# An encoder trunk in fp32: 16 of 22 feed-forward pairs by seven products, and the residual kept in DRAM meanwhile

## The chip, the cores and the metric

The kernel runs on one core of a Trainium2 chip. The metric is the time of one execution on the device in microseconds. The core's engines work side by side, each from its own queue of instructions: TensorE (PE) multiplies matrices, VectorE (DVE) and ScalarE (ACT) do elementwise work, GpSimd (POOL) a little of that, and SyncE (SP) issues most of the transfers from DRAM. The four compute engines see the on-chip memory SBUF; matmuls write to PSUM banks of 128 x 512 fp32.

## The reference: what is computed

A bidirectional encoder of two layers, 512 positions, width 1024. Each layer has two feed-forward half-steps, so there are four of them in the run, and they are what the change touches:

```python
def rmsnorm(x, g):
    xf = x.astype(jnp.float32)
    y = xf * lax.rsqrt(jnp.mean(xf * xf, axis=-1, keepdims=True) + RMS_EPS)
    return (y * g.astype(jnp.float32)).astype(x.dtype)

def swiglu(x, w_gate, w_up, w_down):
    return (jax.nn.silu(x @ w_gate) * (x @ w_up)) @ w_down

    for i in range(DEPTH):
        h = h + 0.5 * swiglu(rmsnorm(h, norm_ffn1[i]), ffn1_w_gate[i], ffn1_w_up[i], ffn1_w_down[i])
        # a mixer: windowed and dilated attention (layer 0), 2-D neighbourhood attention (layer 1)
        h = h + 0.5 * swiglu(rmsnorm(h, norm_ffn2[i]), ffn2_w_gate[i], ffn2_w_up[i], ffn2_w_down[i])
        gate = jax.nn.sigmoid(rmsnorm(h, norm_ple[i]) @ w_ple_gate[i])
        h = h + gate * (p[i] @ w_ple_proj[i])
    return rmsnorm(h, norm_final)
```

The hidden width of the feed-forward is 2816 = 22 x 128.

## The kernel before

Everything lies feature-major: a chunk is 128 features by 512 positions, and the residual h is eight chunks. Precision comes from splitting: every operand is a high part, rounded by ACT (`split`, L123), and a low part, the difference, formed by DVE (L124). A product is three matmuls: high by high, high by low, low by high (`mm3`, L144 to L146).

A feed-forward stage (`ffn`) first goes through 22 pairs. Pair m is 128 columns of the gate and the same 128 of the up matrix: two weight units of 128 x 1024, 512 KB each, which SP loads into a pool of four raw slots (`wr`) and ACT and DVE split into `wh` and `wl`. There are three kinds of pair.

- `pair_front` (m = 0, 1, 2) multiplies the chunks of h times the norm's gain, before the row scale R is known, and multiplies the result by R afterwards (L236, L238). R comes out of squares (L177), a sum over chunks (L182, on POOL), a column sum on PE, a power on POOL and a spread through PE (L208) to ACT (L216).
- `pair` (m = 3, 4 and 15 to 21) multiplies the normalised chunks y: 48 matmuls of 512 columns.
- `pair_fast` (m = 5 to 14) uses the Strassen-Winograd scheme: the 2 x 2 block product (gate and up, by the two halves of the features, by the two halves of the positions) by seven half-size products in place of eight, 84 matmuls of 256 columns. Its weights come as `rs` (one load, and a second one from POOL's queue that adds onto it), `ra` and `rb`; sums of them are formed on DVE (L310, L311) and split. On the other side it needs eight sums of halves of y, `t`, made by `sums` (L276 to L287). Products 1 and 2 go to the two halves of one bank, whose sum is formed by a copy on ACT (L330) and an add on DVE (L331) under high priority; product 5 then accumulates onto the first of them, so it must come after L331. Product 6 uses the split of rb.

The normalised y is formed chunk by chunk by `normal` (L265) after pairs 0 and 1, four chunks each; `sums` forms the same x again from h, gain and R (L276), two of four after pair 2 and two after pair 3. Each result of a pair is split into two slots of the pool `act`. After the pairs the down projection takes three weight units per output chunk, eight outputs, each added to h with a factor 0.5 (L381); the next stage's norm is begun for each chunk as it comes.

Pools set what may be under way at once: 9 slots of residual, 57 of act, 8 of tmp, 4 each of raw, high and low weights. A scheduler orders the instructions of each engine when the program is built, mainly by the program's order and by when slots come free, with some instructions raised by a priority; within an engine the order is then fixed. So the order on DVE, where nearly every split and sum queues, is a product of the pools' sizes as well.

## Time and profile before

| | |
|---|---|
| median of 3 runs | 2135.37 us (2133.22 to 2135.96) |
| the profiled execution | 2134.86 us, span 2133.1 us |
| matmuls on PE | 11390 |
| busy: PE, DVE, ACT, POOL | 97%, 60%, 43%, 14% of the span |
| read from DRAM, written | 223.42 MB, 2.59 MB |

A row of a timeline has the start in us, the duration in us, the engine, the line, the operation, the tiles written and read, and in brackets how long the engine had been idle before it and which instruction ended that. A duration reaches from issue to the end, so those of matmuls overlap; their pace is the distance of two starts. A row of the view by windows has the window, its length, then busy time and count for PE, the weight loads (PEld), DVE, ACT and POOL, the granted PE clock, the share of the DMA engines' time and GB/s. A row of the view of waits has who waited for whom, the total in us, the number of times, the longest.

### The profile page before, as it was taken

The numbers are of one execution on the slowest core, as the hardware profiler recorded it, in microseconds if no ns is written. First come the engines' busy times: TensorE is split into PE (matmuls) and PEld (weight loads), VectorE is DVE, ScalarE is ACT, GpSimd is POOL, SyncE is SP. The second block draws the span as 40 slices with busy tenths as digits, with TensorE's granted clock in tenths as the row PEclk, the third lists the DMA queues.
The fourth block names the chain that finished last, engine by engine and source line by source line (L and its number), as shares of the span: only waits on it lengthen the run. The fifth ranks groups of instructions, "written<-read, shape, count | busy, mean of one in ns | idle before, by whom it ended". The sixth has DMA issues, their size and how long they took to land.

```text
span 2133.1 us, 29295 instructions
## 1 busy us (share of the span) xinstructions
PE 2064.9 (97%) x11390; PEld 1781.0 (83%) x11390; DVE 1289.2 (60%) x2269; ACT 916.2 (43%) x1519; POOL 291.6 (14%) x212
## 2 busy tenths in 40 slices
PE   8999999999999999999999999999999999999998
PEld 6898888777787799888887998888888879988886
DVE  8875332699786887333359873333778777743334
ACT  5454222465534455322344552223656545532232
POOL 3000001233212100001111000013222210000111
PEclk9999999999999999999999999999999999999999
DMA  6574333221222366333333753334333236633331
GB/s 186 133 175 131 91 93 102 85 75 55 65 69 90 88 166 165 109 94 94 106 99 96 181 159 97 92 99 124 103 105 103 81 85 167 164 109 90 101 106 49
DMA packets 86922, 233.71 MB, mean 110 GB/s; under 512 B 18176, under 2 KB 25856, under 8 KB 86784
## 3 DMA queue, kind: packets, MB, share of 16 engines
q1 hardware_dynamic: 80736, 210.78, 32.9%
q0 software_dynamic: 5760, 20.97, 6.0%
q8 instruction: 89, 1.46, 0.3%
q14 instruction: 49, 0.40, 0.1%
q10 hardware_dynamic: 288, 0.10, 0.0%
HBM read 223.42 MB, written 2.59 MB: 106 GB/s over the span
## 4 chain that ended last, share of the span: by engine, by line
PE 76%; DVE 12%; ACT 3%; DMA 3%; issue 2%; POOL 2%; SPq 0%; POOLq 0%; DVEq 0%; ACTq 0%
PE mm L145 10%; PE mm L146 10%; PE mm L144 10%; PE sc L146 7%; PE sc L144 7%; PE sc L145 7%; PE mm L321 3%; PE mm L323 3%; PE mm L322 3%; DVE wl L124 3%; DVE act L124 2%; PE sc L321 1%; PE sc L322 1%; PE sc L323 1%; DMA wr<-in_gu_dram 1%
## 5 line engine op out<-in xcount | busy, mean ns | idle before, releaser
L123 ACT ACTIVATE wh<-wr 128x1024 fp32r<-128x1024 f32 (+1 forms) x400 | 415.0, 1041 | 784.8 <-PE mm L145 286.3
L124 DVE TENSOR_TENSOR wl<-wr,wh 128x1024 fp32r<-128x1024 f32 (+1 forms) x383 | 468.7, 1224 | 385.6 <-ACT wh L123 382.6
L145 PE MATMUL mm<-act,wh 128*128 128x512 f32 x1240 | 485.0, 391 | 2.6 <-DVE act L171 1.6
L144 PE MATMUL mm<-act,wh 128*128 128x512 f32 x1240 | 484.7, 391 | 1.1 <-ACT wh L123 0.8
L146 PE MATMUL mm<-act,wl 128*128 128x512 f32 x1240 | 483.8, 390 | 0.5 <-DVE wl L124 0.5
L146 PE MATMUL sc<-act,wl 128*128 128x512 f32 x818 | 320.3, 392 | 12.4 <-DVE wl L124 12.4
L144 PE MATMUL sc<-act,wh 128*128 128x512 f32 x818 | 320.5, 392 | 0.0
L145 PE MATMUL sc<-act,wh 128*128 128x512 f32 x818 | 320.1, 391 | 0.0
L145 PEld LDWEIGHTS mm<-act,wh 128*128 128x128 f32 x1240 | 233.1, 188 | 51.8 <-DVE act L171 5.1
L144 PEld LDWEIGHTS mm<-act,wh 128*128 128x128 f32 x1240 | 233.1, 188 | 47.7 <-ACT wh L123 1.6
L146 PEld LDWEIGHTS mm<-act,wl 128*128 128x128 f32 x1240 | 233.1, 188 | 46.0 <-DVE wl L124 1.0
L182 POOL TENSOR_TENSOR ssq<-ssq,tmp 128x512 f32<-128x512 f32 x55 | 90.6, 1646 | 977.4 <-ACT tmp L177 950.5
L321 PE MATMUL mm<-act,wh 128*128 128x256 f32 x640 | 183.7, 287 | 15.6 <-DVE tmp L331 15.6
L146 PEld LDWEIGHTS sc<-act,wl 128*128 128x128 f32 x818 | 154.8, 189 | 45.7 <-DVE wl L124 13.6
L145 PEld LDWEIGHTS sc<-act,wh 128*128 128x128 f32 x818 | 154.7, 189 | 32.2
L323 PE MATMUL mm<-act,wl 128*128 128x256 f32 x640 | 181.1, 283 | 0.0
L144 PEld LDWEIGHTS sc<-act,wh 128*128 128x128 f32 x818 | 154.8, 189 | 31.5
L322 PE MATMUL mm<-act,wh 128*128 128x256 f32 x640 | 181.0, 283 | 0.0
L321 PEld LDWEIGHTS mm<-act,wh 128*128 128x128 f32 x640 | 122.6, 192 | 20.3 <-DVE tmp L331 19.6
L123 ACT ACTIVATE act<-tmp 128x512 fp32r<-128x512 f32 x156 | 95.4, 625 | 75.3 <-POOL tmp L239 38.8
L322 PEld LDWEIGHTS mm<-act,wh 128*128 128x128 f32 x640 | 122.7, 192 | 0.2
L323 PEld LDWEIGHTS mm<-act,wl 128*128 128x128 f32 x640 | 122.7, 192 | 0.2
(183 smaller groups left out, 3008.4 us busy)
## 6 DMA issues: line engine op xcount, KB each, us to landing
wr<-in_gu_dram SPq DMA_DIRECT2D x176, 512.0 KB, 3.7
wr<-in_dn_dram SPq DMA_DIRECT2D x64, 512.0 KB, 3.5
wr<-in_gu_dram POOLq DMA_DIRECT2D x40, 512.0 KB, 6.6
wr<-in_dn_dram SPq DMA_DIRECT2D x32, 384.0 KB, 3.1
tmp<-in_gu_dram SPq DMA_DIRECT2D x40, 256.0 KB, 4.3
wr<-in_qk_ab_dram SPq DMA_DIRECT2D x20, 512.0 KB, 3.5
wr<-in_plg_dram SPq DMA_DIRECT2D x16, 512.0 KB, 3.5
wr<-in_qk_c_dram SPq DMA_DIRECT2D x16, 512.0 KB, 3.8
```

The lines of the kernel that those rows point to most:

```text
L123: self.nc.scalar.activation(hi, src, AF.Copy)
L124: (lo_eng or self.nc.vector).tensor_tensor(lo, src, hi.bitcast(F32), op=ALU.subtract)
L144: mm(out, stat[0], mov[0], start=start, stop=False)
L145: mm(out, stat[0], mov[1], start=False, stop=False)
L146: mm(out, stat[1], mov[0], start=False, stop=stop)
L182: eng.tensor_tensor(self.acc, self.acc, sq, op=ALU.add)
L321: mm(out, w[0][:, c], xs[k][0][:, x], start=start and k == 0, stop=False, skip_group_check=True)
L322: mm(out, w[0][:, c], xs[k][1][:, x], start=False, stop=False, skip_group_check=True)
L323: mm(out, w[1][:, c], xs[k][0][:, x], start=False, stop=stop and k == half - 1, skip_group_check=True)
```

## The change

In a feed-forward stage pairs 0 to 3 are now front pairs, 4 and 5 plain, and 6 to 21 go by seven products, 16 in place of 10. `halves(c)` takes the place of `normal` and `sums`: it forms x for chunks c and c + 4 once and makes y[c], y[c + 4] and t[c] from it; it is called after each of the pairs 0 to 3. The raw weight pool has a fifth slot. The residual moves into the act pool, 64 slots; at the start of a stage it is written to DRAM (`kept`; in the first stage the input is there already), and each chunk is loaded again in the down projection. In a front pair the product of gate and up goes from POOL to DVE. In a pair by seven products rb's load is first in the code; the results of products 4 and 6 share a bank, so that two adds of 256 columns (L340, L341) become one of 512 (L353). At the start of the program the first weight unit is loaded in two pieces, the identity matrix later and without its bf16 copy, all eight splits of the input stand ahead of the squares, and the squares are summed on DVE. The mixers' code stays, apart from one tile that moves to the act pool.

```diff
@@ constants and pools
-FRONT = 3
-FAST = 5, 15
+FRONT = 4
+FAST = range(6, 22)
+SUMS = 0, 1, 2, 3
+FIRST = 2
+ACTS = 64
+WR = 5
...
-        self.hp = pool("hres", 9)
-        self.ap_ = pool("act", 57)
+        self.ap_ = pool("act", ACTS)
         self.tp = pool("tmp", 8)
-        self.wr = pool("wraw", 4)
+        self.wr = pool("wraw", WR)
@@ setup
         self.ident = self.cp.tile([P, P], F32, name="ident")
-        nc.scalar.dma_start(self.ident, io["ident"])
-        self.identb = self.cp.tile([P, P], BF16, name="identb")
-        nc.vector.tensor_copy(self.identb, self.ident)
...
-        idle = self.cp.tile([P, T], BF16, name="idle")
+        idle = self.small("R", [P, T], BF16, bufs=1)
...
-        self.h = [None] * KC
+        self.h = []
+        w = io["gu1"][0, 0]
+        units = [(w[:, (1 - j) * UNIT:(2 - j) * UNIT], self.unit_tiles()) for j in range(2)]
+        pieces = {0: (0, 0, UNIT // 4), 1: (0, UNIT // 4, UNIT), 2: (1, 0, UNIT)}
         self.begin_norm(0)
-        for c in range(KC):
-            self.h[c] = self.hp.tile([P, T], F32, tag="h", name=self.nm("h"))
-            nc.sync.dma_start(self.h[c], io["xT"][:, c, :])
-            self.norm_split(c)
-            if c in (0, 2):
-                self.ahead.append(self.unit(io["gu1"][0, 0, :, (1 - c // 2) * UNIT:(2 - c // 2) * UNIT]))
+        for n in range(KC + FIRST):
+            if n < KC:
+                self.h.append(self.act())
+                nc.sync.dma_start(self.h[n], io["xT"][:, n, :])
+                if n in pieces:
+                    j, a, b = pieces[n]
+                    nc.sync.dma_start(units[j][1][0][:, a:b], units[j][0][:, a:b])
+            c = n - FIRST
+            if c >= 0:
+                self.norm_split(c)
+                if c in pieces:
+                    j, a, b = pieces[c]
+                    self.split(*(x[:, a:b] for x in units[j][1]))
+        self.ahead = [u[1:] for _, u in units]
+        nc.sync.dma_start(self.ident, io["ident"])
@@ norm_square
-        nc.scalar.activation(sq, self.h[c], AF.Square)
+        ins = nc.scalar.activation(sq, self.h[c], AF.Square)
+        if self.k == 0:
+            self.tc.keep_in_program_order(ins)
...
-            eng = nc.vector if c == KC - 1 and self.k else nc.gpsimd
+            eng = nc.vector if c == KC - 1 or self.k == 0 else nc.gpsimd
@@ pair_front
-        nc.gpsimd.tensor_tensor(t2, t1, t2, op=ALU.mult)
+        nc.vector.tensor_tensor(t2, t1, t2, op=ALU.mult)
@@ normal and sums become halves
-    def sums(self, y, c):
+    def halves(self, c):
         nc, H = self.nc, T // 2
-        v = []
+        v, out = [], []
         for k in (c, c + KC // 2):
             x = self.tmp()
             nc.vector.scalar_tensor_tensor(x, self.h[k], self.gain[:, self.k, k:k + 1], self.R, op0=ALU.mult, op1=ALU.mult)
+            out.append(self.split_chunk(x, nc.vector))
             v += [x[:, :H], x[:, H:]]
...
-        return [self.split_chunk(x, nc.vector) for x in (s, r)]
+        return (*out, [self.split_chunk(x, nc.vector) for x in (s, r)])
@@ pair_fast
+        dma(rb, w[:, :M])
         dma(rs, w[:, M:M + UNIT])
         nc.gpsimd.dma_start(rs, w[:, :UNIT], accum_op=ALU.add)
         dma(ra, w[:, UNIT:])
-        dma(rb, w[:, :M])
...
-        ab, cd, eb = self.bank(), self.sbank(), self.obank()
-        pa, pb, pc, pd, pe = ab[:, l], ab[:, r], cd[:, l], cd[:, r], eb[:, l]
+        ab, ed, cb = self.bank(), self.sbank(), self.obank()
+        pa, pb, pc, pe, pd = ab[:, l], ab[:, r], cb[:, l], ed[:, l], ed[:, r]
...
-        tt(up[:, l], pe, xy[:, r], op=ALU.add)
-        tt(up[:, r], pd, xy[:, r], op=ALU.add)
+        two = lambda x: x.rearrange("p (a x) -> p a x", a=2)
+        tt(two(up), two(ed), xy[:, r].unsqueeze(1).broadcast_to([P, 2, H]), op=ALU.add)
@@ ffn
+        if first:
+            kept = io["xT"].rearrange("p c t -> c p t")
+        else:
+            kept = self.dp.tile([KC, P, T], F32, name=f"kept_{i}_{which}")
+            for c in range(KC):
+                nc.sync.dma_start(kept[c], self.h[c])
...
-            elif FAST[0] <= m < FAST[1]:
+            elif m in FAST:
...
-            if m < FRONT - 1:
-                n = KC // (FRONT - 1)
-                for c in range(m * n, m * n + n):
-                    y[c] = self.normal(c)
-            elif FRONT - 1 <= m < FAST[0] - 1:
-                n = KC // 2 // (FAST[0] - FRONT)
-                for c in range((m - FRONT + 1) * n, (m - FRONT + 2) * n):
-                    t[c] = self.sums(y, c)
+            for c, after in enumerate(SUMS):
+                if m == after:
+                    y[c], y[c + KC // 2], t[c] = self.halves(c)
         self.begin_norm(k_next)
         for m in range(KC):
+            for c in range(m + 1 if m else 0, min(m + 2, KC)):
+                self.h[c] = self.act()
+                nc.sync.dma_start(self.h[c], kept[c])
```

The lines of the two versions answer to each other so: splits L123, L124 become L136, L137; `mm3` L144 to L146 becomes L160 to L162; L170, L171 become L186, L187; L177, L182 become L193, L200; L216 becomes L234; the front pair's L236, L238, L239 become L254, L256, L257; L276 becomes L287; loads L297 to L300 become L309 to L312; the matmuls of the seven products L321 to L323 become L333 to L335; L330, L331 become L342, L343; L345 becomes L357; L381 becomes L398.

On DVE, within the pairs by seven products of the first stage, the order before reads as follows. L345 ends a pair, `wl<-tmp` is the low part of rb, `wl<-wr` that of a unit of a later product or pair, `act` that of the pair's result:

```order
L124 TENSOR_TENSOR wl_238_1215<-wr_230_1197,wh_237_1214 128x1024
L343 TENSOR_TENSOR tmp_225_1096<-sc_223_1094,tmp_225_1096 128x256
L345 SCALAR_TENSOR_TENSOR tmp_225_1096<-tmp_226_1097,tmp_225_1096 128x512
L124 TENSOR_TENSOR wl_240_1219<-tmp_232_1199,wh_239_1218 128x512
L124 TENSOR_TENSOR wl_253_1334<-wr_249_1326,wh_252_1333 128x1024
L331 TENSOR_TENSOR tmp_244_1225<-mm_241_1222,tmp_244_1225 128x256
L124 TENSOR_TENSOR act_229_1194<-tmp_225_1096,act_228_1193 128x512
L310 TENSOR_TENSOR wr_249_1326<-wr_249_1326,wr_250_1327 128x512
L311 TENSOR_TENSOR wr_249_1326<-wr_249_1326 128x512
```

In this pair two splits stand between L345 and L331; in the next one it is one:

```order
L124 TENSOR_TENSOR wl_257_1344<-wr_249_1326,wh_256_1343 128x1024
L343 TENSOR_TENSOR tmp_244_1225<-sc_242_1223,tmp_244_1225 128x256
L345 SCALAR_TENSOR_TENSOR tmp_244_1225<-tmp_245_1226,tmp_244_1225 128x512
L124 TENSOR_TENSOR wl_259_1348<-tmp_251_1328,wh_258_1347 128x512
L331 TENSOR_TENSOR tmp_263_1354<-mm_260_1351,tmp_263_1354 128x256
L124 TENSOR_TENSOR act_248_1323<-tmp_244_1225,act_247_1322 128x512
```

The wide split `wl_272` stands behind L331 there. The same place after the change, two pairs that follow each other:

```order
L357 SCALAR_TENSOR_TENSOR tmp_268_1403<-tmp_269_1404,tmp_268_1403 128x512
L137 TENSOR_TENSOR act_272_1500<-tmp_268_1403,act_271_1499 128x512
L343 TENSOR_TENSOR tmp_287_1531<-mm_284_1528,tmp_287_1531 128x256
L137 TENSOR_TENSOR wl_283_1525<-tmp_275_1505,wh_282_1524 128x512
L137 TENSOR_TENSOR wl_296_1639<-wr_292_1631,wh_295_1638 128x1024
L322 TENSOR_TENSOR wr_292_1631<-wr_292_1631,wr_293_1632 128x512
L137 TENSOR_TENSOR wl_298_1643<-wr_293_1632,wh_297_1642 128x1024
L351 TENSOR_TENSOR tmp_289_1533<-ob_286_1530,tmp_289_1533 128x256
L323 TENSOR_TENSOR wr_292_1631<-wr_292_1631 128x512
L353 TENSOR_TENSOR tmp_288_1532<-sc_285_1529,tmp_289_1533 128x512
L137 TENSOR_TENSOR wl_300_1649<-wr_292_1631,wh_299_1648 128x1024
L355 TENSOR_TENSOR tmp_287_1531<-sc_285_1529,tmp_287_1531 128x256
```

In the first pair only the result's split is ahead of L343, and rb's has moved behind it. The second pair has rb's and a wide one ahead again:

```order
L357 SCALAR_TENSOR_TENSOR tmp_287_1531<-tmp_288_1532,tmp_287_1531 128x512
L137 TENSOR_TENSOR wl_302_1653<-tmp_294_1633,wh_301_1652 128x512
L137 TENSOR_TENSOR wl_315_1767<-wr_311_1759,wh_314_1766 128x1024
L343 TENSOR_TENSOR tmp_306_1659<-mm_303_1656,tmp_306_1659 128x256
L137 TENSOR_TENSOR act_291_1628<-tmp_287_1531,act_290_1627 128x512
L322 TENSOR_TENSOR wr_311_1759<-wr_311_1759,wr_312_1760 128x512
```

This is the order of seven of the sixteen pairs (11, 13, 15 and 17 to 20); in the others no wide split is ahead of L343, and the order is the same in all four stages.

Also on DVE, the end of the work on the normalised halves in the first stage, ahead of the pairs by seven products. Before, `wl_149` is the second unit of pair 4, behind both of the last sums:

```order
L276 SCALAR_TENSOR_TENSOR tmp_136_596<-h_30_174,gain_93,R_43_253 128x512
L124 TENSOR_TENSOR act_134_591<-tmp_130_581,act_133_590 128x512
L283 TENSOR_TENSOR tmp_137_598<-tmp_135_594 128x256
L285 TENSOR_TENSOR tmp_138_599<-tmp_136_596,tmp_135_594 128x256
L284 SCALAR_TENSOR_TENSOR tmp_137_598<-tmp_137_598,tmp_136_596 128x256
L124 TENSOR_TENSOR wl_149_645<-wr_147_643,wh_148_644 128x1024
L286 SCALAR_TENSOR_TENSOR tmp_138_599<-tmp_137_598,tmp_136_596 128x256
L124 TENSOR_TENSOR act_140_605<-tmp_137_598,act_139_604 128x512
L124 TENSOR_TENSOR wl_158_689<-wr_154_681,wh_157_688 128x1024
```

After, the split in that place is that of the second unit of pair 3, a front pair, with two of the last four splits of halves behind it:

```order
L296 SCALAR_TENSOR_TENSOR tmp_107_485<-tmp_107_485,tmp_104_479 128x256
L137 TENSOR_TENSOR act_103_476<-tmp_101_473,act_102_475 128x512
L297 TENSOR_TENSOR tmp_108_486<-tmp_104_479,tmp_101_473 128x256
L137 TENSOR_TENSOR act_106_482<-tmp_104_479,act_105_481 128x512
L298 SCALAR_TENSOR_TENSOR tmp_108_486<-tmp_107_485,tmp_104_479 128x256
L137 TENSOR_TENSOR wl_119_532<-wr_117_530,wh_118_531 128x1024
L137 TENSOR_TENSOR act_110_492<-tmp_107_485,act_109_491 128x512
L254 TENSOR_TENSOR tmp_121_561<-mm_116_505,R_44_251 128x512
L137 TENSOR_TENSOR act_112_496<-tmp_108_486,act_111_495 128x512
```

From R's first use (L236, L254) there are 59 rows to the first of these splits (`wl_149`) and 40 to the second (`wl_119`).

On SP, the loads for the pairs by seven products, before (L297 rs, L299 ra, L300 rb; their tiles are numbered upwards from pair to pair):

```order
L299 DMA wr_192_939<-in_gu1_dram 128x1024
L297 DMA wr_212_1069<-in_gu1_dram 128x1024
L300 DMA tmp_175_812<-in_gu1_dram 128x512
L299 DMA wr_211_1068<-in_gu1_dram 128x1024
L297 DMA wr_231_1198<-in_gu1_dram 128x1024
L300 DMA tmp_194_941<-in_gu1_dram 128x512
L299 DMA wr_230_1197<-in_gu1_dram 128x1024
```

After (L310 rs, L312 ra, L309 rb):

```order
L312 DMA wr_178_863<-in_gu1_dram 128x1024
L310 DMA wr_198_992<-in_gu1_dram 128x1024
L312 DMA wr_197_991<-in_gu1_dram 128x1024
L309 DMA tmp_161_737<-in_gu1_dram 128x512
L310 DMA wr_217_1120<-in_gu1_dram 128x1024
L312 DMA wr_216_1119<-in_gu1_dram 128x1024
L309 DMA tmp_180_865<-in_gu1_dram 128x512
L310 DMA wr_236_1248<-in_gu1_dram 128x1024
```

A pair's rb stood between rs and ra of two pairs later; it now stands behind both of them.

21 lines of the change are left out of this document (9 added, 12 removed).

## The prediction

> **What bounds the kernel now.** I read the busy shares first, then the chain that ended last, then TensorE's (PE's) waits over the whole run.
>
> ```profile
> PE 2064.9 (97%) x11390; PEld 1781.0 (83%) x11390; DVE 1289.2 (60%) x2269; ACT 916.2 (43%) x1519; POOL 291.6 (14%) x212
> PE 76%; DVE 12%; ACT 3%; DMA 3%; issue 2%; POOL 2%; SPq 0%; POOLq 0%; DVEq 0%; ACTq 0%
> ...
> PE mm L321 <- DVE tmp L331: 15.6, 17, 1.4
> PE sc L146 <- DVE wl L124: 12.4, 4, 3.7
> ...
> PE mm L145 <- DVE act L171: 1.6, 4, 0.7
> ```
>
> PE is busy 97% of the span and holds 76% of the chain, so time goes down in two ways only: fewer or shorter matmuls, or less of PE waiting. The two largest waits both end on VectorE (DVE) inside the feed-forward stages, and both stand at places that the change rewrites: the copy-and-add L331 in the pairs by seven products, and the low part of a weight unit (L124) just ahead of them.
>
> The pace of the matmuls comes from the timeline of PE, from the first and the last row of an unbroken run of each kind.
>
> ```profile
> 32.21 0.39 PE L145 MATMUL mm<-act,wh 128*128 128x512 f32 x1
> ...
> 41.95 0.39 PE L146 MATMUL mm<-act,wl 128*128 128x512 f32 x1
> ...
> 81.03 0.28 PE L321 MATMUL ob<-act,wh 128*128 128x256 f32 x1
> ...
> 88.35 0.28 PE L322 MATMUL sc<-act,wh 128*128 128x256 f32 x1
> ```
>
> The first two are 43 matmuls apart: 9.74 / 43 = 0.2265 us each. The others are 61 apart: 7.32 / 61 = 0.120 us. A plain pair has 48 of the wide ones, 10.87 us; a pair by seven products has 84 of the narrow ones, 10.08 us. Each pair that changes kind saves 0.80 us of PE, if nothing new waits.
>
> **The pairs by seven products, as they run now.** They do not run at 10.08. The first row below is one of the matmuls that waited, the second the next such, two pairs later; the third is that stretch by engine.
>
> ```profile
> 122.26 0.39 PE L321 MATMUL mm<-act,wh 128*128 128x256 f32 x1 [1.20 <-DVE tmp L331]
> ...
> 143.79 0.39 PE L321 MATMUL mm<-act,wh 128*128 128x256 f32 x1 [1.11 <-DVE tmp L331]
> ...
> 122.00:143.70 21.70, 20.42 (x168) 20.21 (x168) 17.33 (x28) 11.73 (x19) 1.71 (x2) 1.00 0.70 171
> ```
>
> Two pairs take 143.79 - 122.26 = 21.53 us against 20.16: 1.37 lost, of which 1.1 shows as a wait and the rest is a slow restart. With 15.6 us in the view of waits, that scales to 15.6 x 1.37 / 1.11 = 19; by the sum of all start-to-start gaps above 0.120 it is 21 us over 40 pairs, 0.53 a pair, the figure I use. It is not throughput: in the same stretch DVE works 17.33 of 21.70. It is order. Product 5 may not start before L331 has read its bank, 4 x 12 x 0.120 = 5.76 us after the pair's start. The timeline of DVE shows a pair that kept this date and the next, that missed it:
>
> ```profile
> 107.87 0.69 DVE L345 SCALAR_TENSOR_TENSOR tmp<-tmp,tmp 128x512 f32<-128x512 f32 x1 [0.70 <-ACT tmp L344]
> 109.42 0.69 DVE L124 TENSOR_TENSOR wl<-tmp,wh 128x512 fp32r<-128x512 f32 x1 [0.85 <-ACT wh L123]
> 110.03 0.42 DVE L331 TENSOR_TENSOR tmp<-mm,tmp 128x256 f32<-128x256 f32 x1
> ...
> 118.64 0.69 DVE L345 SCALAR_TENSOR_TENSOR tmp<-tmp,tmp 128x512 f32<-128x512 f32 x1 [0.70 <-ACT tmp L344]
> 119.70 0.69 DVE L124 TENSOR_TENSOR wl<-tmp,wh 128x512 fp32r<-128x512 f32 x1 [0.36 <-ACT wh L123]
> 120.64 1.23 DVE L124 TENSOR_TENSOR wl<-wr,wh 128x1024 fp32r<-128x1024 f32 x1 [0.26 <-ACT wh L123]
> 121.79 0.42 DVE L331 TENSOR_TENSOR tmp<-mm,tmp 128x256 f32<-128x256 f32 x1
> ```
>
> The second has a 1.23 us split of the next unit ahead of L331. Ahead of that stands the split of rb, which waits for its hi part on ScalarE (ACT), and that for a load:
>
> ```profile
> 114.65 1.07 SPq L300 DMA_DIRECT2D tmp<-in_gu_dram  x1
> ...
> 119.03 0.63 ACT L123 ACTIVATE wh<-tmp 128x512 fp32r<-128x512 f32 x1 [0.42 <-DMA tmp<-in_gu_dram]
> ```
>
> Issued at 114.65, used at 119.03: 4.4 us. So the chain is rb's load, ACT, two splits, L331.
>
> **The change, part by part.** (a) *Start.* Now the first pair waits for the low parts of x (L171, the 1.6 us above and the slow run of DVE behind it).
>
> ```profile
> 0.00:24.50 24.50, 20.09 (x60) 10.76 (x61) 17.62 (x17) 15.73 (x23) 11.80 (x11) 0.93 0.64 223
> ...
> 7.39 0.50 PE L144 MATMUL mm<-act,wh 128*128 128x512 f32 x1 [0.79 <-ACT wh L123]
> ...
> 24.35 0.40 PE L146 MATMUL sc<-act,wl 128*128 128x512 f32 x1
> 24.58 0.61 PE L189 MATMUL tr<-ones,ssq 128*128 128x1 f32 x5
> ...
> 6.61 0.74 DVE L171 SCALAR_TENSOR_TENSOR act<-h,gain,act 128x512 fp32r<-128x512 f32 x1
> ...
> 13.10 8.57 DVE L171 SCALAR_TENSOR_TENSOR act<-h,gain,act 128x512 fp32r<-128x512 f32 x5
> ...
> 12.24 8.87 POOL L182 TENSOR_TENSOR ssq<-ssq,tmp 128x512 f32<-128x512 f32 x5 [0.15 <-ACT tmp L177]
> ...
> 29.13 0.69 DVE L236 TENSOR_TENSOR tmp<-mm,R 128x512 f32<-128x512 f32 x1 [2.26 <-ACT R L216]
> ...
> 14.28 0.61 ACT L177 ACTIVATE tmp<-h 128x512 f32<-128x512 f32 x1
> ...
> 15.93 0.71 ACT L170 ACTIVATE act<-h,gain 128x512 fp32r<-128x512 f32 x1
> ...
> L123 ACT ACTIVATE wh<-wr 128x1024 fp32r<-128x1024 f32 (+1 forms) x400 | 415.0, 1041 | 784.8 <-PE mm L145 286.3
> ```
>
> One L171 alone takes 0.74; five beside GpSimd's (POOL's) L182 take 8.57, 1.71 each, while ACT had its last part ready at 16.64. The change takes L182 off POOL and puts the squares behind the splits. The five then cost 5 x 0.74 = 3.7, 4.9 less, and the squares' 0.61 us each leave ACT's way. Without waits, 48 matmuls from 7.39 end at 18.3; the pair now ends at 24.35 + 0.23 = 24.6. I take -6; if x's arrival decides (the share of DMA is 0.64 here) -2; at best -7.5, with an earlier start from the first weights' smaller piece. The identity matrix, now loaded behind part of x, is wanted only for spreading R, after 25; the cast that is dropped stood beside other work.
> The Trainium skill, "SBUF — State Buffer", section "Who interferes with whom", says that a VectorE instruction with two SBUF inputs contends with a GpSimd instruction that reads SBUF. L171 and L182 are such a pair, and 0.74 against 1.71 agrees; by that rule the seven adds on DVE give the 4.9 back in full, the upper part of my term.
>
> (b) *Entry.* Four times the pairs by seven products begin late, behind DVE's queue after the scale R is known:
>
> ```profile
> 68.31 0.50 PE L146 MATMUL sc<-act,wl 128*128 128x512 f32 x1 [1.93 <-DVE wl L124]
> ...
> 698.31 0.60 ACT L216 ACTIVATE R<-tr 128x512 f32<-128x512 f32 x1
> ...
> 740.00 0.58 PE L146 MATMUL sc<-act,wl 128*128 128x512 f32 x1 [3.16 <-DVE wl L124]
> 740.37 0.63 PE L144 MATMUL sc<-act,wh 128*128 128x512 f32 x1
> ...
> 699.00:740.00 41.00, 37.84 (x170) 31.21 (x168) 37.02 (x62) 20.92 (x31) 6.32 (x5) 1.00 0.34 84
> 740.00:744.00 4.00, 4.00 (x11) 3.14 (x12) 4.00 (x6) 0.63 (x1) 0.00 (x0) 0.57 0.45 131
> ```
>
> From R to the end of that window DVE has 62 instructions, 37.02 us, 0.60 each; PE's 170 matmuls last 38.5. The wait is followed by 4.00 us at a granted clock of 0.57 with 11 starts in them, ten intervals in place of 17.6: 7.6 x 0.2265 = 1.7 us more. 12.4 + 3 x 1.7 = 17.5; by start-to-start gaps 2.2, 5.3, 5.1 and 5.5, together 18. After the change each x is formed once and split once, and the queue from R to the low part of the second unit of pair 3, the split that now stands behind this work, is 40 instructions: 40 x 0.60 = 24, with one wide split and more 0.69s 26 us. PE has 128 matmuls in that time, 29 us. Stages 2 to 4 lose 0.4 each, for the last y. In the first stage R comes late: 8 splits, 8 squares and 3 weight parts on ACT (8 x 0.71 + 8 x 0.61 + 3 x 1.04 = 13.7, from about 7) end near 20.7; the last add, 0.7, and the 29.13 - 24.58 = 4.55 that the steps from the sum to R take now put it near 26, 3 us sooner, while the first pair ends 6 sooner. Of PE's 29 us of cover 8 are then gone, 21 against 26, less the 2 us or so that PE loses by itself while it waits for R: 3.5 us of wait are left there. 18 - 4.7 = 13.3 gained; ends 0 (DVE is no sooner) and 17. The product of gate and up, moved from POOL to DVE, adds 0.69 a pair, counted in the 26; uncovered it would be 4 x 4 x 0.69 = 11.
>
> (c) *Kind of pair.* 6 more in each of 4 stages, 24 x 0.80 = -19.2.
> By the Trainium skill, "TensorE: Matmul & The Clock Gate", section "Back-to-back issue gap", the isolated gap is N/2.4 + 2.5 ns, 215.8 and 109.2 ns for these widths: an estimate of 24 x 1.19 = -28.5 in place of -19.2, and a time near 2081. No chance is given to it, since both intervals stand measured above at a granted clock of 1.00.
>
> (d) *Waits in these pairs.* 40 x 0.53 = 21 become 64 x s. The new order has the wide split ahead of the copy-and-add (now L343) in pairs 11, 13, 15 and 17 to 20: seven in sixteen, against four in ten. But the fifth raw slot lets the big loads go about 8 us sooner, so those splits no longer wait for their data; rb is issued behind the ra of two pairs on. With the durations above I replayed DVE's queue in its new order: in a row of pairs with the wide split ahead, the copy-and-add ends 4.2 to 4.6 us after the pair's start, within 5.76; where such a pair follows one without it, 0 to 0.5 late. One add of 512 columns for two of 256 saves 2 x 0.42 - 0.69 = 0.15 a pair. POOL issues its accumulating load for 24 more pairs; it is busy 1.71 of 21.70 and has lost its adds, so nothing is queued ahead of them. My replay leaves out jitter of the loads, so I take s = 0.2, 12.8 us: -8. Ends: s = 0.05, -18; s = 0.53 as now, +13.
>
> (e) *The residual in DRAM.* Three times eight 256 KB writes at a stage's start and four times eight reads in the down projection, two outputs ahead at the start and one later. A down stage has room:
>
> ```profile
> 255.00:355.00 100.00, 100.00 (x443) 82.79 (x442) 32.32 (x34) 27.28 (x33) 9.05 (x5) 1.00 0.32 96
> ```
>
> A load of that size, rb's, took 4.4 us; an output's 66 matmuls are 15 us. If one came late, it would first delay L398 on DVE, then the norm's chunks queued behind it. A write waits for its own chunk; SP's loads behind it are for pairs two later. I count nothing; uncovered, 4.4 us for each stage's first read, at most 18. For the passage from pair 21, whose delayed splits now stand together, I add 1.5 (0 to 6).
>
> Sum: -6 - 13.3 - 19.2 - 8 + 1.5 = -45.0. The profiled execution took 2134.9 (span 2133.1), the median is 2135.4: **2090**. Own range, 2078 to 2100.
>
> **The rivals.** *B: the waits stay.* Order alone decides, and s is 0.53: 64 x 0.53 - 12.8 = 21 more, **2111**. For it: more wide splits stand ahead of the copy-and-add. Against: what the rows show waiting there is the data of rb and the wide unit, and both loads move. *C: the waits go* (s = 0.05, 9.6 less; the entries at their best, 3.7 less): **2077**. *D: slower.* The tmp slots run out. The results of pairs 16 to 20 stay in tmp until the act slots are free, so eight of eight are taken when rb of pair 21 is wanted; if rb's load is issued only when its product is due, each such pair waits 4.4 + 0.63 + 0.69 = 5.7 us. From 45 / 5.7 = 8 pairs in all on nothing is gained; with 16 (pairs 18 to 21 of each stage) +91, **2181**. Against: by count they fit. *E: the entries stay as they are*, since the halves' instructions run slower in one row than the mean 0.60: 13.3 back, **2103**.
>
> **How the numbers follow.** Forecast 0.54, B 0.19, C 0.12, D 0.08, E 0.07. B, C and E all lie on the faster side; of D a quarter ends near no change. A measurement of this kernel tells about 0.2% (4 us) from no change: faster 0.92, same 0.02, slower 0.06. The range of 8 in 10 takes in E, B and most of C: 2073 to 2113.
>
> **What would show it.** In the changed profile: the first pair ends near 18 and L186's mean is near 0.74; the wait of PE for a weight's low part falls from 12.4 to under 5; the wait for L343 is 5 to 15 us over 64 pairs, with two pairs 20.2 to 20.8 us apart; PE's matmuls rise by 24 x 36 = 864; no wait on L391. The forecast is wrong if two pairs still take 21.5, or if waits on rb's split appear at pairs 18 to 21.

## The result, and the profile after

The changed kernel takes 2110.6 us (median of 4 runs, 2109.96 to 2113.26) against 2134.3 for the one before on the same chip: ratio 0.9891, 95% interval 0.9874 to 0.9908. It is 23.7 us faster. The forecast was 45 us, 2090. The sign held, and the time lies inside the range of 8 in 10 (2073 to 2113) but outside the forecast's own (2078 to 2100); the gain is about half of the one forecast.

Of the page and the view of TensorE's waits, the rows that answer to those shown before:

```profile
PE 2043.4 (97%) x12254; PEld 1807.9 (86%) x12254; DVE 1382.1 (66%) x2416; ACT 983.8 (47%) x1640; POOL 282.7 (13%) x217
PE 84%; DVE 8%; issue 4%; ACT 3%; POOL 1%; DMA 1%; SPq 0%; DVEq 0%; ACTq 0%; POOLq 0%
...
PE mm L333 <- DVE tmp L343: 25.1, 19, 2.6
...
PE mm L160 <- ACT act L186: 2.5, 1, 2.5
...
PE sc L162 <- DVE wl L137: 0.7, 1, 0.7
```

The matmuls rose by 864, as the change says. The wait at the entry of the pairs by seven products fell from 12.4 us to 0.7. The wait for the copy-and-add, now L343, did not fall: 25.1 us in 19 waits, where it was 15.6 in 17. Summed over the gaps between starts above 0.120 us, the 64 pairs lose 9.5, 8.2, 5.7 and 10.6 us in the four stages, 34.0 together or 0.53 a pair, the rate before the change. Two pairs that still take 21.5 us were named as a sign that the forecast is wrong: two take 21.4, 21.3, 20.9 and 21.6 us in the mean of the four stages, and 22.9 in the stretch below.

One of the longest of these waits, in pair 11 of the first stage, which starts at 132.0, by the timelines of SP, POOL, ACT, DVE and PE:

```profile
131.05 0.33 SPq L312 DMA_DIRECT2D wr<-in_gu_dram  x1
131.43 0.50 SPq L309 DMA_DIRECT2D tmp<-in_gu_dram  x1
...
129.06 0.86 POOL L311 DMA_DIRECT2D wr<-in_gu_dram  x1 [10.99 <-DMA wr<-in_gu_dram]
...
137.20 0.63 ACT L136 ACTIVATE wh<-tmp 128x512 fp32r<-128x512 f32 x1 [1.81 <-DMA tmp<-in_gu_dram]
...
135.42 0.69 DVE L357 SCALAR_TENSOR_TENSOR tmp<-tmp,tmp 128x512 f32<-128x512 f32 x1 [0.70 <-ACT tmp L356]
137.87 0.69 DVE L137 TENSOR_TENSOR wl<-tmp,wh 128x512 fp32r<-128x512 f32 x1 [1.75 <-PE sc L334]
138.81 1.22 DVE L137 TENSOR_TENSOR wl<-wr,wh 128x1024 fp32r<-128x1024 f32 x1 [0.25 <-ACT wh L136]
139.95 0.42 DVE L343 TENSOR_TENSOR tmp<-mm,tmp 128x256 f32<-128x256 f32 x1
...
140.43 0.38 PE L333 MATMUL mm<-act,wh 128*128 128x256 f32 x1 [2.46 <-DVE tmp L343]
...
132.00:154.90 22.90, 20.44 (x170) 20.24 (x170) 17.57 (x25) 12.31 (x19) 1.73 (x2) 1.00 0.65 170
```

rb's load goes out 0.38 us behind ra, 0.6 ahead of the pair's start, and ACT has it at 137.20, 5.8 us later; in the pair shown before the change it was 4.4 us. DVE has nothing to do from 136.1 to 137.9, since its next instruction is the split of rb, and the wide split and L343 stand behind it. The bracket at 137.87 names a matmul, but ACT's high part of rb ended at 137.83; in all the pairs where this split waits, it starts 0.03 us after ACT's end. L343 ends 8.4 us after the pair's start, and its date is 5.76. The window by engines shows that DVE had time enough: 17.57 of 22.90.

This pair is one of the worst. In the traces as a whole, rb's split and a wide one stand ahead of L343 in the 28 pairs 11, 13, 15 and 17 to 20 of the four stages, and these lose 29 of the 34 us, 1.0 each. In them rb lands 3.5 us after the pair's start in the mean (2.0 to 5.3), and where L343 is late it ends 3.2 us after the landing. Before the change 16 pairs had that order; rb landed 3.5 us after the start there too, and they lost 15 us, 0.95 each. So such a pair is no worse than before, and there are more of them. Pairs 7 to 9 and 21 have rb's split alone ahead of L343 and lose next to nothing. Pair 6 has both splits ahead, which the section on the change leaves out, but its rb lands 0.8 to 2.5 us before the pair's start, and L343 is in time in all four stages. In the first, where pair 6 starts at 81.41:

```profile
85.50 1.22 DVE L137 TENSOR_TENSOR wl<-wr,wh 128x1024 fp32r<-128x1024 f32 x1 [1.74 <-ACT wh L136]
86.64 0.42 DVE L343 TENSOR_TENSOR tmp<-mm,tmp 128x256 f32<-128x256 f32 x1
```

The start, by the timelines of PE, DVE and ACT, and the entry of the first stage:

```profile
9.62 0.79 PE L160 MATMUL mm<-act,wh 128*128 128x512 f32 x1 [2.46 <-ACT act L186]
...
15.52 0.63 PE L161 MATMUL mm<-act,wh 128*128 128x512 f32 x1
15.94 0.60 PE L162 MATMUL mm<-act,wl 128*128 128x512 f32 x1
...
12.34 2.07 DVE L187 SCALAR_TENSOR_TENSOR act<-act,gain,act 128x512 fp32r<-128x512 f32 x3
...
22.92 0.68 DVE L200 TENSOR_TENSOR ssq<-ssq,tmp 128x512 f32<-128x512 f32 x1
...
27.31 0.95 PE L207 MATMUL tr<-ones,ssq 128*128 128x1 f32 x8
...
31.22 0.60 ACT L234 ACTIVATE R<-tr 128x512 f32<-128x512 f32 x1 [0.37 <-PE tr L226]
...
55.71 0.50 PE L162 MATMUL sc<-act,wl 128*128 128x512 f32 x1 [0.68 <-DVE wl L137]
```

PE starts early, runs out of data, waits 2.46 us, and then has its matmuls 0.43 apart until 16, at a granted clock of 0.50. The 48th wide matmul of the program starts at 23.2 (24.3 before), the 96th at 36.5 (37.9 before): 1.1 to 1.4 us gained. In the profiles of six of the kernels below, which have the same start, the 96th comes at 35.0 to 36.8, so this place scatters by nearly 2 us. R is ready at 31.8, later than the 29.1 before: the last square is added at 23.6, but the matmuls that sum it over the partitions (L207) stand in PE's queue behind the first seventeen of pair 1 and run at 27.31.

The residual's way through DRAM shows in no wait. The down stage runs as it did, PE busy without a gap:

```profile
255.00:355.00 100.00, 100.00 (x443) 82.83 (x442) 32.14 (x34) 27.74 (x34) 9.05 (x5) 1.00 0.39 122
```

### The profile page after: what moved, and what is told of

Same layout as the page of the kernel before. It is cut to its first block, busy times and chain, and to the rows that moved or that the text cites. A ratio compares the mean times of both kernels' runs of the same rounds, so it can differ in the third digit from the quotient of the medians.

```text
span 2108.2 us, 31604 instructions
## 1 busy us (share of the span) xinstructions
PE 2043.4 (97%) x12254; PEld 1807.9 (86%) x12254; DVE 1382.1 (66%) x2416; ACT 983.8 (47%) x1640; POOL 282.7 (13%) x217
## 4 chain that ended last, share of the span: by engine, by line
PE 84%; DVE 8%; issue 4%; ACT 3%; POOL 1%; DMA 1%; SPq 0%; DVEq 0%; ACTq 0%; POOLq 0%
PE mm L161 9%; PE mm L162 9%; PE mm L160 9%; PE sc L160 6%; PE sc L162 6%; PE sc L161 6%; PE mm L333 6%; PE mm L335 6%; PE mm L334 6%; PE sc L333 3%; PE sc L334 3%; PE sc L335 3%; PE ob L333 1%; PE ob L334 1%; PE ob L335 1%
## 5 line engine op out<-in xcount | busy, mean ns | idle before, releaser
L136 ACT ACTIVATE wh<-wr 128x1024 fp32r<-128x1024 f32 (+2 forms) x425 | 441.5, 1040 | 659.9 <-PE mm L161 210.0
L137 DVE TENSOR_TENSOR wl<-wr,wh 128x1024 fp32r<-128x1024 f32 (+2 forms) x408 | 496.5, 1219 | 339.5 <-ACT wh L136 333.9
L160 PE MATMUL mm<-act,wh 128*128 128x512 f32 (+1 forms) x1048 | 410.9, 393 | 2.8 <-ACT act L186 2.5
L161 PE MATMUL mm<-act,wh 128*128 128x512 f32 (+1 forms) x1048 | 411.2, 392 | 1.1 <-POOL act L137 0.6
L162 PE MATMUL mm<-act,wl 128*128 128x512 f32 (+1 forms) x1048 | 410.0, 391 | 0.0
L333 PE MATMUL mm<-act,wh 128*128 128x256 f32 x1024 | 293.6, 287 | 25.4 <-DVE tmp L343 25.1
L335 PE MATMUL mm<-act,wl 128*128 128x256 f32 x1024 | 290.0, 283 | 0.0
L334 PE MATMUL mm<-act,wh 128*128 128x256 f32 x1024 | 289.9, 283 | 0.0
L162 PE MATMUL sc<-act,wl 128*128 128x512 f32 x626 | 243.7, 389 | 0.7 <-DVE wl L137 0.7
L160 PE MATMUL sc<-act,wh 128*128 128x512 f32 x626 | 244.3, 390 | 0.0
L161 PE MATMUL sc<-act,wh 128*128 128x512 f32 x626 | 243.9, 390 | 0.0
L160 PEld LDWEIGHTS mm<-act,wh 128*128 128x128 f32 x1048 | 197.8, 189 | 41.8 <-ACT act L186 2.9
L161 PEld LDWEIGHTS mm<-act,wh 128*128 128x128 f32 x1048 | 197.9, 189 | 41.4 <-DVE act L137 1.8
L162 PEld LDWEIGHTS mm<-act,wl 128*128 128x128 f32 x1048 | 197.7, 189 | 37.8
L333 PEld LDWEIGHTS mm<-act,wh 128*128 128x128 f32 x1024 | 196.4, 192 | 30.7 <-DVE tmp L343 30.3
L334 PEld LDWEIGHTS mm<-act,wh 128*128 128x128 f32 x1024 | 196.7, 192 | 0.2
L335 PEld LDWEIGHTS mm<-act,wl 128*128 128x128 f32 x1024 | 196.6, 192 | 0.0
L200 POOL TENSOR_TENSOR ssq<-ssq,tmp 128x512 f32<-128x512 f32 x48 | 79.2, 1649 | 696.8 <-ACT tmp L193 670.2
L334 PE MATMUL sc<-act,wh 128*128 128x256 f32 x512 | 145.5, 284 | 0.0
L333 PE MATMUL sc<-act,wh 128*128 128x256 f32 x512 | 145.5, 284 | 0.0
L335 PE MATMUL sc<-act,wl 128*128 128x256 f32 x512 | 145.4, 284 | 0.0
```

The lines of the kernel that those rows point to most:

```text
L136: self.nc.scalar.activation(hi, src, AF.Copy)
L137: (lo_eng or self.nc.vector).tensor_tensor(lo, src, hi.bitcast(F32), op=ALU.subtract)
L160: mm(out, stat[0], mov[0], start=start, stop=False)
L161: mm(out, stat[0], mov[1], start=False, stop=False)
L162: mm(out, stat[1], mov[0], start=False, stop=stop)
L200: eng.tensor_tensor(self.acc, self.acc, sq, op=ALU.add)
```

## The experiments

**Where the 34 us come from.** Theory 1: rb lands late, its split stands ahead of the copy-and-add in DVE's queue. Theory 2: the wide split, or the amount of work on DVE. The first edit takes rb out of the tmp pool:

```diff
+        self.wb = pool("wrb", 2)
...
-        rb = self.tmp()
+        rb = self.wb.tile([P, T], F32, tag="rb", name=self.nm("rb"))
```

> The changed kernel with one edit: rb gets a pool of two slots of its own, so that its load no longer waits for a tmp slot, and SP issues it a pair earlier; rb's split is then done before the end of the pair ahead, and only the wide split of the next unit stands ahead of L344 (the copy-and-add, L343 in the change). Theory 1 (the waits come from rb's late landing, its split standing ahead of the copy-and-add): the 25.1 us of waits fall under 5, the 34 us lost in the pairs by seven products under 6, time near 2081. Theory 2 (the wide split, or the sheer amount of work on VectorE, is what makes the copy-and-add late): the wide split is now ahead of it in all pairs, so the waits stay at 25 or grow, time 2108 or more.

Measured: 2079.0 us (2076.45 to 2079.78), ratio to before 0.9746 (0.9726 to 0.9765), 31.6 less than the change. The wait on the copy-and-add is gone from the list; the four stages lose 0.8 us each. The timelines of SP and DVE, and a window of two pairs:

```profile
112.47 0.33 SPq L310 DMA_DIRECT2D rb<-in_gu_dram  x1
119.59 0.33 SPq L313 DMA_DIRECT2D wr<-in_gu_dram  x1
...
122.61 0.33 SPq L310 DMA_DIRECT2D rb<-in_gu_dram  x1
129.72 0.33 SPq L313 DMA_DIRECT2D wr<-in_gu_dram  x1
...
132.03 0.68 DVE L138 TENSOR_TENSOR wl<-rb,wh 128x512 fp32r<-128x512 f32 x1
...
133.75 0.69 DVE L358 SCALAR_TENSOR_TENSOR tmp<-tmp,tmp 128x512 f32<-128x512 f32 x1 [0.70 <-ACT tmp L357]
135.20 1.23 DVE L138 TENSOR_TENSOR wl<-wr,wh 128x1024 fp32r<-128x1024 f32 x1 [0.77 <-ACT wh L137]
136.35 0.42 DVE L344 TENSOR_TENSOR tmp<-mm,tmp 128x256 f32<-128x256 f32 x1
...
131.10:151.40 20.30, 20.30 (x171) 20.30 (x170) 16.97 (x25) 11.80 (x18) 1.72 (x2) 1.00 0.68 179
```

The rb of the pair that starts at 131.1 is issued at 112.47, 18.6 us ahead of it (the load at 122.61 is that of the next pair, 141.2, since the pool has two slots), and it is split at 132.03, before L358 ends the pair ahead. The wide split still stands ahead of the copy-and-add, here as in 15 of the 16 pairs of a stage, and the copy-and-add ends 5.7 us after the start, just in time. Theory 2 falls. The pairs follow each other every 10.13 us (119.59, 129.72).

Was it the slot, or the place in SP's queue? Two more tmp slots leave both orders as they are:

```diff
-        self.tp = pool("tmp", 8)
+        self.tp = pool("tmp", 10)
```

> The changed kernel with ten tmp slots in place of eight and nothing else; the order on VectorE and SP stays. It tells which part of the edit with rb's own slots matters. Theory 1a (rb's load waits in SP's queue behind ra of two pairs on, and that for a raw slot): no change, 2110 within 4, waits on the copy-and-add 22 to 28 us. Theory 1b (rb's load waits for its tmp slot): the load goes earlier, waits under 10, time near 2090.

Measured: 2112.25 us (2109.82 to 2116.59), ratio 0.9906 (0.9882 to 0.9929), as the change itself; the wait remains:

```profile
PE mm L333 <- DVE tmp L343: 26.7, 17, 2.7
```

So a free tmp slot is not what rb's load waits for: its place in SP's queue, which is fixed, is the same as in the change. The next edit gives the fifth raw slot back, which puts rb's load ahead of ra again, as it was before the change, with the order on DVE unchanged:

```diff
-WR = 5
+WR = 4
```

> The changed kernel with four raw slots in place of five. The order on VectorE is the same in the pairs by seven products; on SP rb's load stands between rs and ra of two pairs on, as before the change. Theory 1a: the seven pairs with rb's split ahead of the copy-and-add lose about 1.3 us each, as before the change (1.37 per such pair), 4 x 7 x 1.37 = 38 us against 34 now: time 2110 to 2117. If the fifth slot is what keeps VectorE's splits fed: many more waits, 2125 or more.

Measured: 2098.91 us (2096.59 to 2102.04), ratio 0.9842 (0.9821 to 0.9863): 12 us faster than the change, better than either theory said; the pairs by seven products lose 21 us in place of 34. The wait, and the pair that answers to the one above:

```profile
PE mm L333 <- DVE tmp L343: 13.4, 24, 1.7
...
131.47 0.33 SPq L310 DMA_DIRECT2D wr<-in_gu_dram  x1
131.85 0.78 SPq L309 DMA_DIRECT2D tmp<-in_gu_dram  x1
...
135.96 0.63 ACT L136 ACTIVATE wh<-tmp 128x512 fp32r<-128x512 f32 x1
...
138.72 0.42 DVE L343 TENSOR_TENSOR tmp<-mm,tmp 128x256 f32<-128x256 f32 x1
```

Here rb is in use 4.1 us after its issue in place of 5.8. Over the 28 pairs it lands 2.9 us after the start in place of 3.5, and they lose 15 us in place of 29. My price for such a pair, 1.37 us, was too high; they lose 0.55 in the mean and 1.85 at most. The fifth slot costs this kernel 12 us. The same slot alone, put into the kernel before:

```diff
-        self.wr = pool("wraw", 4)
+        self.wr = pool("wraw", 5)
...
-        idle = self.cp.tile([P, T], BF16, name="idle")
+        idle = self.small("R", [P, T], BF16, bufs=1)
```

> The kernel before with a fifth raw slot alone (and the start's idle tile in R's place, to make room). On SP rb's load moves behind ra of two pairs on, as in the changed kernel; VectorE's order stays. Theory 1a: rb lands later against the pair's start, each wait on L331 grows from about 1.0 to 1.5 to 2.5 us, total from 15.6 to 20 or more, time 2136 to 2145. If the fifth slot helps by itself because the big loads go earlier: waits under 10, time 2122 to 2130.

Measured: 2152.04 us (2149.28 to 2155.08), ratio 1.0086 (1.0062 to 1.011), slower by 18 to 19 us, more than the upper end. A wait in pair 9 of the first stage, as in the change:

```profile
PE mm L321 <- DVE tmp L331: 25.3, 20, 2.8
...
119.63 0.33 SPq L299 DMA_DIRECT2D wr<-in_gu_dram  x1
120.01 0.49 SPq L300 DMA_DIRECT2D tmp<-in_gu_dram  x1
...
125.93 0.63 ACT L123 ACTIVATE wh<-tmp 128x512 fp32r<-128x512 f32 x1 [1.96 <-DMA tmp<-in_gu_dram]
...
130.00:133.30 3.30, 3.30 (x18) 3.30 (x17) 2.46 (x4) 0.38 (x1) 0.00 (x0) 0.50 0.80 153
```

rb is in use 5.9 us after its issue behind ra, and the matmul that waited starts at 129.16. The waits grew by 9.7 us, which is half of the 19. Most of the rest is in the last row: after five of these waits the granted clock is 0.50 for 3.41 us, which costs 1.7 us each time; in the kernel before that follows none of them. Then the cure alone in the kernel before:

```diff
+        self.wb = pool("wrb", 2)
...
-        rb = self.tmp()
+        rb = self.wb.tile([P, T], F32, tag="rb", name=self.nm("rb"))
...
-        idle = self.cp.tile([P, T], BF16, name="idle")
+        idle = self.small("R", [P, T], BF16, bufs=1)
```

> The kernel before the change with nothing but rb's two slots of its own (and the start's idle tile in R's place, to make room). If rb's late landing is also what the 15.6 us of waits before the change came from: they fall under 3, the 21 us in these pairs nearly all go, 2134 - 20 = 2114, and this edit alone gains about as much as the whole change. If the pairs before the change waited for another reason (four raw slots, the wide splits): 2125 or more.

Measured: 2118.55 us (2113.84 to 2119.81), ratio 0.992 (0.9901 to 0.9939). The wait on L331 is off the list and the entry's is first again:

```profile
PE sc L147 <- DVE wl L125: 11.9, 4, 3.4
```

16 us from this small edit; the whole change brought 24. It lies between the 2114 and the 2125 of the two readings, nearer the first, and the loss in these pairs fell from 21 us to 3. And in the changed kernel with rb's own slots, four raw slots in place of five:

```diff
+        self.wb = pool("wrb", 2)
...
-WR = 5
+WR = 4
```

> The kernel with rb's own slots (2079 us) with four raw slots in place of five. If the fifth slot mattered only by pushing rb's load back: the same time, 2075 to 2083, no waits on the copy-and-add. If it feeds the splits as well: waits come back on the low parts of rs and ra, 2086 or more.

Measured: 2077.43 us (2075.83 to 2077.84), ratio 0.973 (0.9714 to 0.9746). There is no difference to five slots that these runs can tell: the order on DVE is the same, and once rb has its own slots the fifth raw slot gives nothing.

**The entry.** In `halves` x is formed a second time, as it was before:

```diff
             out.append(self.split_chunk(x, nc.vector))
+            x = self.tmp()
+            nc.vector.scalar_tensor_tensor(x, self.h[k], self.gain[:, self.k, k:k + 1], self.R, op0=ALU.mult, op1=ALU.mult)
             v += [x[:, :H], x[:, H:]]
```

> The changed kernel, but the halves' sums form x a second time, as the kernel before did: eight more instructions of 0.69 to 0.74 us on VectorE between R and the entry of the pairs by seven products in each stage. Theory (the entry waits went because VectorE's queue after R now ends ahead of TensorE's cover): 8 x 0.7 = 5.6 us more of queue; the first stage, which has no slack (0.7 us of wait), waits 5 to 6 us, stages 2 to 4 wait 0 to 3 each since some slack is there; time 2116 to 2126. Rival (the waits went because the weight splits moved ahead in the queue, not because there is less work): no wait on a weight's low part above 1 us, 2110 within 4.

Measured: 2115.86 us (2110.95 to 2120.36), ratio 0.9904 (0.9881 to 0.9928). The first stage waits again, the others don't:

```profile
57.78 0.50 PE L162 MATMUL sc<-act,wl 128*128 128x512 f32 x1 [4.11 <-DVE wl L137]
```

The time alone does not part the two readings, the intervals overlap; the row does: 4.11 us of wait in place of 0.68, for 5.6 us more work in the queue. Where R is early (stages 2 to 4) there is slack for all of it.

**The start.** The old start in the changed kernel, with the identity on ACT's queue; the first unit is loaded in one piece again, and the squares are neither held back nor summed on DVE:

```diff
-        for n in range(KC + FIRST):
...
+        for c in range(KC):
+            self.h[c] = self.act()
+            nc.sync.dma_start(self.h[c], io["xT"][:, c, :])
+            self.norm_split(c)
+            if c in (0, 2):
+                self.ahead.append(self.unit(io["gu1"][0, 0, :, (1 - c // 2) * UNIT:(2 - c // 2) * UNIT]))
...
-        if self.k == 0:
-            self.tc.keep_in_program_order(ins)
...
-            eng = nc.vector if c == KC - 1 or self.k == 0 else nc.gpsimd
+            eng = nc.vector if c == KC - 1 and self.k else nc.gpsimd
```

> The changed kernel with the start as before the change: first unit in one piece, squares between the splits and summed on GpSimd. My prediction's term for the start, -6, would give 2116 or more here. By the place of the 96th wide matmul (36.5 us in the changed kernel, 37.9 before) the start is worth 1.4: 2112, with the instructions that form x's low parts at 1.7 us each again and the first pairs' matmuls waiting for them.

Measured: 2127.8 us (2124.72 to 2131.42), ratio 0.9963 (0.995 to 0.9977): 17 us slower than the change, far beyond both numbers. Its rows, from the waits, ACT, DVE and SP, and a window by engines:

```profile
PE mm L151 <- DVE wl L126: 6.1, 2, 5.5
PE sc L149 <- DVE tmp L243: 5.6, 1, 5.6
...
35.17 0.60 ACT L221 ACTIVATE R<-tr 128x512 f32<-128x512 f32 x1 [2.40 <-PE tr L213]
...
13.81 1.79 DVE L176 SCALAR_TENSOR_TENSOR act<-act,gain,act 128x512 fp32r<-128x512 f32 x1
16.05 0.75 DVE L176 SCALAR_TENSOR_TENSOR act<-act,gain,act 128x512 fp32r<-128x512 f32 x1 [0.45 <-ACT act L175]
...
25.86 0.72 ACT L175 ACTIVATE act<-act,gain 128x512 fp32r<-128x512 f32 x1 [1.98 <-DMA act<-in_xT_dram]
...
22.68 0.60 SPq L118 DMA_DIRECT2D act<-in_xT_dram  x1
...
50.00:63.60 13.60, 4.65 (x10) 3.31 (x11) 13.60 (x22) 4.19 (x7) 0.00 (x0) 0.50 0.15 47
```

Its first pairs are not slower (the 96th wide matmul starts at 35.2). What is late is x: its last chunk is in use at 25.9, and so R is ready at 35.8, 4 us behind the change, and PE waits 5.6 us for the banks that R frees and 5.5 for a weight's low part behind them, at a granted clock of 0.50. The first pair by seven products starts 11.4 us later than in the change, out of 15.8 between the two spans. x is late because SP issues its eight chunks one by one between loads of weights and of the mixers' tables, the last at 22.68. In the change all were out by 9.1, and in the kernel before by 7.3:

```profile
3.07 4.20 SPq L116 DMA_DIRECT2D h<-in_xT_dram  x5
```

So this run does not price the old start: in the changed kernel much the same lines give another order on SP. Which part of the change does that was not separated. The row at 13.81 shows the old contention: 1.79 us while POOL adds, 0.75 alone.

Then more idle matmuls for TensorE in the changed kernel:

```diff
-WARM = 12
+WARM = 24
```

> The changed kernel with 24 idle matmuls at the start in place of 12. In the changed kernel the first real matmul comes at 6.1 us, the next group at 9.6, and up to 16.4 us the matmuls are 0.43 apart at a granted clock below 1. Theory (the start gained little since the matmuls that were there early ran at the low clock, after a wait of 2.5 us for data): with TensorE kept busy until the data is there, the real matmuls start near 10 to 11 us, run 0.2265 apart, and the 96th is at 33.5 to 35.5 in place of 36.5; 2 us gained, 2108. Rival (x's arrival sets the end of the first pair): no earlier than 36.5, time 2110 to 2113.

Measured: 2109.04 us (2101.23 to 2109.76), ratio 0.9865 (0.9843 to 0.9887); not told from the change by its time. The real matmuls start later and then run at full pace:

```profile
9.27 0.58 PE L160 MATMUL mm<-act,wh 128*128 128x512 f32 x1
9.69 0.39 PE L161 MATMUL mm<-act,wh 128*128 128x512 f32 x1
9.92 0.39 PE L162 MATMUL mm<-act,wl 128*128 128x512 f32 x1
```

The 48th starts at 21.1 in place of 23.2, the 96th at 34.6 in place of 36.5. In the change's profile the granted clock is 0.50 from 9.6 to 16.4, here it is 1.00 from 9 to 40, so the 2 us did go to the low clock. Against the six other kernels with twelve idle matmuls, whose low clock at the start lasts 3.4 to 6.8 us, the gain is 0.4 to 2.3 us.

**A pair's worth.** With rb's own slots, pairs 16 to 21 made plain again:

```diff
+        self.wb = pool("wrb", 2)
...
-FAST = range(6, 22)
+FAST = range(6, 16)
```

> The kernel with rb's own slots (2079 us, no waits in the pairs by seven products), with ten such pairs in a stage (6 to 15) in place of sixteen. It measures what a pair's change of kind is worth when nothing waits. By the rows' pace, 24 x 0.80 = 19.2 us more: 2098. By an isolated gap of N/2.4 + 2.5 ns, which the Trainium skill (TensorE: Matmul & The Clock Gate, section Back-to-back issue gap) states, an estimate of 28.5 more: 2107.5.

Measured: 2095.78 us (2094.06 to 2098.96), ratio 0.9816 (0.9796 to 0.9835): 16.8 us for 24 pairs, 0.70 each (15.2 and 0.63 if each of the two is taken against the kernel before on its own chip). The steps of 10.13 us above against 10.87 give 0.74 and 17.8. The estimate of 28.5 us from the isolated gap of the Trainium skill (TensorE: Matmul & The Clock Gate, Back-to-back issue gap) does not hold here.

**Together.** rb's own slots and 24 idle matmuls, and the same with pair 5 by seven products too (the edit of `FAST` is in the second alone):

```diff
+        self.wb = pool("wrb", 2)
...
-WARM = 12
+WARM = 24
...
-FAST = range(6, 22)
+FAST = range(5, 22)
```

> rb's own slots together with 24 idle matmuls at the start. The two act in different places, so 2079 - 2 = 2077, with the 96th wide matmul near 34.5 us.

> As the last one, with pair 5 by seven products too (17 in a stage). If the halves are ready by the end of pair 4, 4 x 0.70 to 0.80 less: 2074. If they are not, a wait of TensorE for the halves' parts or for a weight's low part of 1 us or more shows at the entry of each stage, 2077 or more.

Measured: 2077.16 us (2076.32 to 2078.02), ratio 0.973 (0.9715 to 0.9745), and 2074.81 us (2072.88 to 2077.52), ratio 0.9723 (0.9704 to 0.9742). Both have no wait on the copy-and-add and none over 1 us at the entry. In the first the idle matmuls' gain does not show (the 96th at 35.7, against 35.6 without them): the clock is 0.50 from 27.8 to 31.1 in this profile, which costs 1.7 us there. The second is the fastest run here, 60 us under the kernel before and 36 under the change; against 2077 its interval does not tell it apart.

## Why the prediction was right or wrong

By its own terms, each beside what the profiles of before and after give:

| term | forecast | measured |
|---|---|---|
| (a) start | -6 | -1.4 (96th matmul 37.9 to 36.5; by other profiles of the same start up to -2.9) |
| (b) entry | -13.3 | -17 (waits 12.4 to 0.7, and three spells of 1.7 at the low clock gone) |
| (c) kind of pair | -19.2 | -18 (24 x 0.74 to 0.76) |
| (d) waits in the pairs | -8 | +13 (21 to 34) |
| (e) residual, passage | +1.5 | about 0 |
| sum | -45 | -23.4, of 24.9 between the two spans |

**(d) is the step that failed**, in the sentence that the fifth raw slot lets the big loads go sooner and that the copy-and-add then ends 4.2 to 4.6 us after the pair's start. The order on DVE was as read. What I had in hand and priced wrong was the row on SP: rb is issued behind the ra of two pairs on. From rb's landing to the end of L343 it is 3.2 us by the durations of the rows (ACT 0.63, DVE 0.69, 1.22 and 0.42, and what lies between), so 4.2 to 4.6 would have needed rb 1.0 to 1.4 us after the start. It landed at 3.5 in the mean of these pairs, as before the change, and in the pair shown at 5.1, with L343 ending at 8.4. How the replay came to its figure is not on record; the forecast's own row, 4.4 us from issue to use, is already too long for it, since rb is issued only 1.3 us ahead of these pairs in the mean (0.9 before the change). What the big loads bring sooner does no good while DVE's next instruction waits for the small one. The runs settle the cause: taking rb's load out of that place takes 31 of the 34 us away (2079), giving the slot back takes 13 (2099), giving more room without moving the load takes nothing (2112).

The measured time is that of **rival B**, 2111, to which I gave 0.19. Its price for (d), 0.53 a pair, came out, and half of its reason: more pairs have the wide split ahead, 28 in place of 16, and each loses what such a pair lost before. But order alone does not decide. With rb early the wide split stands ahead of the copy-and-add in 15 of 16 pairs and nothing waits; it takes both, the order and the late rb. I argued against B that both loads move; rb's did not come sooner against its pair. That the figure agrees so closely is partly luck: the profile with ten tmp slots has the same orders and loses 43 us, 0.67 a pair, as a low clock follows five of its waits and only one in the change's. The total's agreement is partly luck too: the start gave 4.6 less and the entry 3.7 more than its sum took. Rival C, without waits, was 2077; the kernel takes 2079 once rb has its slots.

**(a) was mis-sized.** L171 did go from 1.71 to about 0.7 us, as the rows and the rule of the Trainium skill (SBUF — State Buffer, Who interferes with whom) said; L187 takes 2.07 us for three in the change. (The forecast's last paragraph names L186, which is ACT's part; L187 is the one meant.) But I put the first pair at 48 matmuls times 0.2265 from 7.39, at full clock, though the window that I quoted has a granted clock of 0.93: some 14 matmuls at the low clock cost 3 us here, and the wait for x's second chunk 2.5. R came 2.7 us later and not 3 sooner, because I took the partition sum to follow the last add, and it stands behind seventeen matmuls of pair 1 in PE's queue. **(b)** came out larger, as stages 2 to 4 have slack and not 0.4 us of loss, and the first waited 0.7 for the 3.5 (its own terms, 26 - 21 - 2, give 3.0). There two errors cancelled: R came 5.8 us later than the 26 forecast, but the first pair also ended 5.2 later than the 18.3. **(c)** was right to 7% by the steps and 13% by the run with ten such pairs. **(e)**: no wait, as argued; at the passage from pair 21 the next matmul starts 0.12 us after the last in all four stages. Rival D (tmp slots) did not happen; two more slots change nothing. Rival E did not happen.

## What to carry to other kernels

A deeper pool for the big operand moves the small one: with a queue in order, ask of each load what now stands ahead of it, and of each wait whether its data come late or its engine is busy. Where an engine with a third of its time free still makes another wait, look for the instruction in its queue that waits for data, and give that operand slots of its own before adding any to the others. A saving per unit that is worked out from an undisturbed stretch is only as good as the stretch; here more than half of it (13 of 18 us) was lost to a wait that cost two lines to remove.

## What the runs showed that I had not expected

The two slow loads of rb shown here, 5.8 and 5.9 us to their use behind ra, and the faster ones, 4.1 and 4.4 behind rs, are single cases. Over all its loads rb takes 4.5 us from issue to landing in the change (3.4 to 6.2) and 4.0 with four raw slots (3.3 to 5.2); in the kernel before it is 4.2, with a fifth slot 4.6. What goes with the long ones is POOL's accumulating load: it is under way during 53 of 64 of rb's loads in the change and during 18 of 64 with four slots, and within each of these kernels such loads are slower than the others (4.6 against 4.1 and 4.3 against 3.9 us). Whether that overlap or ra itself makes the difference was not tried.

A wait can cost more than its length. In the eight traces with waits on the copy-and-add, 43 of these waits are longer than 1.6 us; at 19 of them the granted clock goes to 0.50 for 3.41 or 6.83 us, and at none of the shorter ones. What decides between the 19 and the other 24 the traces don't show.

The fifth raw slot made both kernels slower, by 12 and by 18 to 19 us.
